# Running sums kept in one PSUM bank: the Winograd products of an output projection and an up projection

## The chip, the cores and the metric

The kernel runs on one NeuronCore of a Trainium2 chip. The metric is the device time of one execution in microseconds (us). Before the change it is 2968.75 us, the median of three runs (2968.43 to 2971.05).

The names of the engines are those of the profile: PE is the matrix engine (TensorE), PEld its weight loads, DVE the vector engine (VectorE), ACT the scalar engine (ScalarE), POOL GpSimd, and SP the engine whose queue issues most of the DMA transfers.

## The reference, cut to what matters

One layer of a hybrid encoder block for 512 tokens and a model width of 2048, in float32:

```
y  = RMSNorm(x) @ W_in                       # two recurrent groups of heads are fed from y
h  = x + concat[GDN(y), RWKV7(y)] @ W_out    # the output projection ("op")
h += CrossAttn(RMSNorm(h), RMSNorm(mem))
h += squared_relu(RMSNorm(h) @ W_up) @ W_down   # "up": 2048 -> 8192, "down": 8192 -> 2048
out = RMSNorm_final(h)
```

The change touches the two products `mixed @ W_out` (2048x2048) and `hn @ W_up` (2048x8192).

## The kernel before

Everything is held transposed: a tile has 128 features on the partitions and the 512 tokens along its free dimension. A float32 operand is split into two rounded parts, `hi` and `lo` (`split`, L130 and L131: ACT writes `hi`, DVE writes `lo = a - hi`), and a product is `hi·hi + hi·lo + lo·hi`, all three added up in PSUM.

Output projection and up are made of **units**: 8 units `op0` to `op7` and 32 units `up0` to `up31`, each a call of `strassen`. One unit makes a 256-feature by 512-token output. It is worked as a Winograd form of the 2x2 block product: the output is two feature halves (index 0 and 1) by two token halves, `HA` (tokens 0 to 255) and `HB` (256 to 511). Seven products replace eight. A product is named after its activation side, `B11`, `T1`, `T2`, `T3`, `T4`, `B22` or `B21`. That side lies ready in `comb[i][k]`, eight tiles of 512 columns: the `hi` part of 256 tokens in the first half, the `lo` part in the second. The weight side is one of the four blocks a11, a12, a21, a22 of 128x1024, loaded by DMA (L1305), or a combination of them: s1 = a21 + a22, s2 = s1 - a11, s4 = a12 - s2, and a11 - a21. DVE makes the combinations, and each product's weight side is then split by ACT and DVE.

A product is 24 multiplications of 128x128 by 256 columns. In `product` it is issued in one of two forms:

- **narrow**: for each of eight k, `hi` weights times `comb[:, HA]`, then the same weights times `comb[:, HB]`, both into the same 256 columns of the bank; then eight times `lo` weights times `comb[:, HA]`. 24 matmuls of 256 columns.
- **wide**: for each k, `hi` weights times all 512 columns of `comb`, into all 512 columns of the bank, so that two partial sums lie side by side; then the eight `lo` matmuls of 256 columns into the first half. 8 + 8 matmuls. Whoever reads the product must add both halves.

Units up1 to up30 are wide in all products; op1 to op6 in B11, T2 and T3 alone; op0, op7, up0 and up31 are narrow throughout.

Every product has a bank of its own. DVE adds the products up in SBUF, 256 columns at a time (`add`, L1336, one operand in PSUM): u1 = P1, u2 = u1 + P6, u3 = u2 + P7 and so on. A wide unit has 15 such additions and one ACT copy out of PSUM (L1354). `done` is called for each half tile as it is finished: in up it squares the ReLU on ACT and stores the tile (L1713 to L1716); in op it adds the input x and collects the sum of squares.

What sets the order: PE, DVE, ACT and SP each work through a queue in program order and wait on semaphores. In these stages the queues' order is made by the scheduler of the language layer when the program is built, from its own estimates, and not by the order of the source lines. Loaded blocks live in rotating buffers: `wraw` has three (a11 and a21 of each unit take turns in it), `wraw2` three (a22 and a12), `whi` and `wlo` two each, `ws` two. A load into a buffer waits for the last reader of what was in it.

Of the kernel before, what the change touches and what calls it, by code (L numbers as in the profile page):

```python
# [11 lines left out]
AF = mybir.ActivationFunctionType  # L12
ALU = mybir.AluOpType
# [4 lines left out]
P = 128  # L18
# [55 lines left out]
def build(tc, I, out):  # L74
    nc = tc.nc
# [42 lines left out]
    def psb(nm, tag="mx", bufs=2):  # L118
        return tile_of(ps, [P, 512], F32, tag, nm, bufs)

    def mm(o, l, r, start=True, stop=True):
        PE.matmul(o, l, r, start=start, stop=stop)  # L122

    def rsq(o, x, scale, eps):
        S.activation(o, x, AF.Ln, bias=eps, scale=scale)
# [1125 lines left out]
    def sl2(w=512):  # L1251
        cnt[0] += 1
        return ph.tile([P, 512], F32, tag="sl", name=f"sl{cnt[0]}", bufs=3)[:, 0:w]
# [17 lines left out]
    def sub(o, a, b):  # L1271
        V.tensor_tensor(out=o, in0=a, in1=b, op=ALU.subtract)
# [7 lines left out]
    def differ(i, e, o):  # L1280
        if i == T1:
            sub(e[:, HA], e[:, HB], e[:, HA])
        elif i == T2:
            sub(e[:, HA], o[:, HB], e[:, HA])
        elif i == T3:
            sub(e[:, HB], o[:, HB], e[:, HB])
        elif i == T4:
            sub(e[:, HA], e[:, HA], o[:, HA])

    def block(i, e, o):  # L1290
        return o[:, HB] if i == B22 else o[:, HA] if i == B21 else e[:, HB] if i == T3 else e[:, HA]

    def strassen(nm, pool, src, ks, done, used=None, first=False, wide=(), sums=None):

        w = len(ks) * P

        def raw(p_, tag, bufs, i):  # L1300
            cnt[0] += 1
            r = p_.tile([P, 1024], F32, tag=tag, name=f"{tag}_{cnt[0]}", bufs=bufs)[:, 0:w] \
                if p_ is pw else p_.tile([P, pool[1]], F32, tag=tag, name=f"{tag}_{cnt[0]}", bufs=bufs)[:, 0:w]
            if i is not None:
                nc.sync.dma_start(r, src[i])  # L1305
            return r

        def product(i, tag, a):
            cnt[0] += 1
            hi = pw.tile([P, 1024], F32R, tag="whi", name=f"whi{cnt[0]}", bufs=NWS)[:, 0:w]  # L1310
            lo = pw.tile([P, 1024], F32R, tag="wlo", name=f"wlo{cnt[0]}", bufs=NWS)[:, 0:w]
            split(a, hi, lo)
            pt = psb(f"{nm}_{i}", tag)
            pa_ = pt[:, HA]
            last = len(ks) - 1
            for zs in (range(last), range(last, last + 1)) if first else (range(last + 1),):
                for z in zs:
                    k, sl = ks[z], slice(z * P, z * P + P)
                    if i in wide:
                        mm(pt, hi[:, sl], comb[i][k], start=z == 0, stop=False)  # L1320
                    else:
                        mm(pa_, hi[:, sl], comb[i][k][:, HA], start=z == 0, stop=False)
                        mm(pa_, hi[:, sl], comb[i][k][:, HB], start=False, stop=False)
                for z in zs:
                    mm(pa_, lo[:, z * P:z * P + P], comb[i][ks[z]][:, HA], start=False, stop=z == last)
            if used:
                used(i)
            return (pa_, pt[:, HB]) if i in wide else (pa_,)

        def plus(o, a, p, op=ALU.add):  # L1330
            for x in p:
                add(o, a, x, op)
                a = o

        def add(o, a, b, op=ALU.add):
            V.tensor_tensor(out=o, in0=a, in1=b, op=op)  # L1336

        def wraw2(i):
            return raw(pool[0], "wraw2", 3, i)

        def ws():
            return raw(pool[0], "ws", 2, None)

        a11 = raw(pw, "wraw", NWR, 0)
        if first:
            a12, a22 = raw(pw, "wraw", NWR, 3), raw(pw, "wraw", NWR, 2)
            a21 = wraw2(1)
        else:
            a21 = raw(pw, "wraw", NWR, 1)
            a22, a12 = wraw2(2), wraw2(3)  # L1350
        p1 = product(B11, "mx", a11)
        c1 = sums[0] if sums else sl2()
        c11, c12 = u1, u4 = c1[:, HA], c1[:, HB]
        S.copy(u1, p1[0])  # L1354
        for x in p1[1:]:
            add(u1, u1, x)
        if first:
            p2 = product(B21, "mg", a12)
            p4 = product(T4, "mx", a22)
        s1 = ws()  # L1360
        add(s1, a21, a22)
        p5 = product(T1, "mg", s1)
        s2 = ws()
        add(s2, s1, a11, ALU.subtract)
        p6 = product(T2, "mm", s2)
        c2 = sums[1] if sums else sl2()
        c21, c22 = u3, u2 = c2[:, HA], c2[:, HB]
        plus(u2, u1, p6)
        if first:
            plus(c11, u1, p2)  # L1370
        plus(u4, u2, p5)
        add(a21, a11, a21, ALU.subtract)
        p7 = product(T3, "mm", a21)
        plus(u3, u2, p7)
        plus(c22, u3, p5)
        done(1, HB, c2)
        if not first:
            p4 = product(T4, "mx", a22)
        plus(c21, u3, p4, ALU.subtract)
        done(1, HA, c2)  # L1380
        s4 = ws()
        add(s4, a12, s2, ALU.subtract)
        p3 = product(B22, "mg", s4)
        plus(c12, u4, p3)
        done(0, HB, c1)
        if not first:
            p2 = product(B21, "mm", a12)
            plus(c11, u1, p2)
        done(0, HA, c1)

# [10 lines left out]
    def spread(*which):  # L1403
        for i, k in which:
            comb[i][k] = (btile if k < 3 or i == B21 and k < 6 else act_tile)(f"ob{i}_{k}")
            place(i, k, *pair[k])
# [114 lines left out]
    for p in range(8):  # L1521
        xs = [None, None]

        def used(i):
            if i == T1:
                if p == 0:
                    spread((B22, 6), (B22, 7))
                for j in (1, 0):
                    xs[j] = sl2()
                    nc.sync.dma_start(xs[j], I["xT"][:, 2 * p + j, :])  # L1530
            elif i == T2 and p == 0:
                spread((B21, 6), (B21, 7))
                sqsum.append(ph.tile([P, T], F32, tag="acc", name="acc1", bufs=1))
            if p == 7 and i in (T2, T3):
                for n in range(2) if i == T2 else range(2, 4):
                    second(n)

        def gained(j, half, c):
            if half is HB:
                return  # L1540
            V.tensor_tensor(out=c, in0=c, in1=xs[j], op=ALU.add)
            acc = sqsum[0]
            if p == 0 and j:
                S.activation(acc, c, AF.Square)
            else:
                sq = sl2()
                S.activation(sq, c, AF.Square)
                V.tensor_tensor(out=acc, in0=acc, in1=sq, op=ALU.add)

        strassen(f"op{p}", (pz, 1024), [I["w_out"][p, i] for i in range(4)], list(range(8)), gained, used,  # L1550
                 wide=(B11, T2, T3) if 0 < p < 7 else (), sums=hres[2 * p:2 * p + 2])
    pz_cm.__exit__(None, None, None)
    pl_cm = tc.tile_pool(name="pl", bufs=1, reuse_waits="tile")
    pl = pl_cm.__enter__()
# [153 lines left out]

    ahead = []
    for p in range(32):  # L1710
        def square(i, half, c):
            t = c[:, half]
            S.activation(t, t, AF.Relu)  # L1713
            S.activation(t, t, AF.Square)
            if half is HA:
                nc.scalar.dma_start(Ud[p][:, i, :], c)  # L1716

        def used(i):
            if p == 0 and i == B21:
                pt = psb("pss2")  # L1720
                mm(pt, ones, acc)
                V.tensor_scalar(out=rstd, in0=pt, scalar1=1.0 / 2048, scalar2=1e-6, op0=ALU.mult, op1=ALU.add)
            if 3 < p < 8 and i == T1:
                c = slice((p - 4) * P, (p - 3) * P)
                V.reciprocal(out=rstd[:, c], in_=rstd[:, c])
            if 7 < p < 16 and i in (B11, T3):
                f = p - 8
                if i == B11:
                    ahead.append(pu.tile([P, T], F32, tag="ur", name=f"ua{f}", bufs=1))
                    nc.sync.dma_start(ahead[f], Ud[f // 2][:, f % 2, :])  # L1730
                else:
                    V.tensor_tensor(out=ahead[f], in0=ahead[f], in1=rstd, op=ALU.mult)
                    nc.scalar.dma_start(Ud[f // 2][:, f % 2, :], ahead[f])
            if p == 31 and i in (T1, T2, T3):
                for f in (range(0, 3), range(3, 6), range(6, 8))[i - T1]:
                    usplit(f)

        strassen(f"up{p}", (pu, 1024), [I["w_up"][p, i] for i in range(4)], list(range(8)), square, used, p == 0,
                 range(7) if 0 < p < 31 else ())


    dcomb = {e: {i: [] for i in (T1, T2, T3, T4)} for e in range(1, 7)}
# [211 lines left out]
    pt = psb("pss4")  # L1954
# [126 lines left out]
```

## Time and profile before

| what | value |
|---|---|
| median of three runs | 2968.75 us |
| the profiled execution, first to last instruction | 2967.1 us |
| PE busy | 2938.2 us (99%) |
| DVE busy | 2323.9 us (78%) |
| ACT busy | 1520.1 us (51%) |
| stage op, first to last matmul | 1294.6 to 1455.4 us |
| stage up, first to last matmul | 1634.9 to 2263.2 us |

The span of the profiled execution is the time from its first to its last instruction. It is 1.65 us under the median of the three runs. In a row of a timeline the first column is the start in us from the start of the span, then the length in us, the engine, the source line, the operation, and what it writes from what; "x8" are eight instructions merged in one row, and brackets tell how long the engine had been idle and what ended that. The ends of matmuls are modelled and overlap the next start, so the pace of PE is read from starts. In a row of a group the busy time of the whole group stands behind the bar, then the mean duration of one in ns.

### The profile page before, as it was taken

The page shows a single profiled execution, that of the slowest core. Times are in us where ns is not written, and L with a number is a line of the kernel's source. Part 1 is how long each engine was busy: PE and PEld are TensorE (multiplying, and loading weights), DVE is VectorE, ACT ScalarE, POOL GpSimd, SP SyncE. Part 2 cuts the span into 40 slices and gives each one's busy share as a digit, 9 for nine tenths or more (in the row PEclk, how much of TensorE's full clock was granted, in tenths as well). Part 3 has the DMA queues.
Part 4 walks back from the last instruction along what each step waited for, and adds up shares of the span by engine and source line. Part 5 has one row for each costly group of instructions (what it writes and reads, how often), then busy time and mean ns, then how long its engine had stood idle before and what let it go on. Part 6 is the DMA issues. An engine that isn't in the chain of part 4 may idle for free.

```text
span 2967.1 us, 51025 instructions
## 1 busy us (share of the span) xinstructions
PE 2938.2 (99%) x20106; PEld 2515.2 (85%) x20106; DVE 2323.9 (78%) x3725; ACT 1520.1 (51%) x2271; POOL 215.2 (7%) x552
## 2 busy tenths in 40 slices
PE   9999999999999999999999999999999999999998
PEld 7877887887788888889988988888888888998887
DVE  7677676676778667679748999999999688888777
ACT  6455555555556555654436555555555343343334
POOL 0212302302312000000000000000000000000000
PEclk9999999999999999999999999999999999999999
DMA  5333332333435587864323445444445334333436
GB/s 179 111 87 85 101 93 81 102 92 82 132 89 166 168 278 250 259 231 136 100 86 100 146 153 170 136 142 135 136 135 177 110 108 139 128 114 114 135 121 185
DMA packets 229312, 407.35 MB, mean 137 GB/s; under 512 B 92168, under 2 KB 115980, under 8 KB 229072
## 3 DMA queue, kind: packets, MB, share of 16 engines
q1 hardware_dynamic: 212944, 375.77, 41.0%
q10 hardware_dynamic: 16128, 28.32, 2.6%
q8 instruction: 158, 2.59, 0.4%
q14 instruction: 82, 0.67, 0.1%
HBM read 354.32 MB, written 49.69 MB: 136 GB/s over the span
## 4 chain that ended last, share of the span: by engine, by line
PE 86%; DVE 6%; DMA 4%; POOL 2%; issue 2%; ACT 1%; SPq 0%; ACTq 0%; DVEq 0%; POOLq 0%
PE up L122 21%; PE py L251 20%; PE dn L122 14%; PE op L122 5%; PE d L122 4%; PE vp L122 3%; PE at L122 3%; PE sc L122 3%; PE kp L251 3%; PE kq L251 2%; DVE wlo L131 2%; POOL sr L251 2%; DVE h L1810 1%; PE vo L122 1%; DMA wraw<-in_wqT 1%
## 5 line engine op out<-in xcount | busy, mean ns | idle before, releaser
L130 ACT CAST whi<-wraw 128x1024 fp32r<-128x1024 f32 x372 | 391.4, 1052 | 567.6 <-PE dn L122 189.9
L131 DVE TENSOR_TENSOR wlo<-wraw,whi 128x1024 fp32r<-128x1024 f32 x372 | 453.9, 1220 | 64.4 <-ACT whi L130 60.9
L122 PE MATMUL up<-cb,whi 128*128 128x512 f32 (+1 forms) x1904 | 451.4, 380 | 0.0
L251 PE MATMUL py<-xhi,whi 128*128 128x512 f32 x928 | 374.2, 403 | 6.6 <-ACT xhi L251 6.6
L122 PEld LDWEIGHTS up<-cb,whi 128*128 128x128 f32 x1904 | 330.7, 189 | 54.9 <-issue 0.2
L251 PE MATMUL py<-xlo,whi 128*128 128x512 f32 x928 | 374.2, 403 | 0.0
L251 PE MATMUL py<-xhi,wlo 128*128 128x512 f32 x928 | 373.6, 403 | 0.1
L251 ACT CAST whi<-wraw 128x1024 fp32r<-128x1024 f32 (+1 forms) x180 | 188.0, 1044 | 211.9 <-PE py L251 133.1
L251 DVE TENSOR_TENSOR wlo<-wraw,whi 128x1024 fp32r<-128x1024 f32 (+1 forms) x180 | 220.9, 1227 | 87.7 <-ACT whi L251 86.5
L122 PEld LDWEIGHTS up<-cb,wlo 128*128 128x128 f32 x1792 | 244.1, 190 | 16.4
L122 PE MATMUL up<-cb,wlo 128*128 128x256 f32 x1792 | 251.1, 282 | 0.0
L122 PE MATMUL dn<-uh,whi 128*128 128x512 f32 x640 | 244.7, 391 | 0.8 <-ACT whi L130 0.8
L122 PE MATMUL dn<-ul,whi 128*128 128x512 f32 (+1 forms) x648 | 244.7, 388 | 0.0
L122 PE MATMUL dn<-uh,wlo 128*128 128x512 f32 (+1 forms) x640 | 235.1, 367 | 0.0
L251 PEld LDWEIGHTS py<-xhi,whi 128*128 128x128 f32 x928 | 175.3, 189 | 41.6 <-ACT xhi L251 7.0
L1336 DVE TENSOR_TENSOR sl<-sl,up 128x256 f32<-128x256 f32 x464 | 182.0, 414 | 35.0 <-PE up L122 31.8
L251 PEld LDWEIGHTS py<-xlo,whi 128*128 128x128 f32 x928 | 175.2, 189 | 37.3 <-issue 3.3
L251 PEld LDWEIGHTS py<-xhi,wlo 128*128 128x128 f32 x928 | 175.2, 189 | 35.2 <-issue 1.0
L130 ACT CAST whi<-ws 128x1024 fp32r<-128x1024 f32 x120 | 126.1, 1051 | 108.7 <-PE up L122 70.4
L1972 POOL TENSOR_TENSOR h<-h,rstd 128x256 f32<-128x256 f32 x5 | 3.4, 724 | 2012.6 <-ACT rstd L1966 2012.6
L131 DVE TENSOR_TENSOR wlo<-ws,whi 128x1024 fp32r<-128x1024 f32 x120 | 146.0, 1218 | 0.5 <-ACT whi L130 0.5
L122 PEld LDWEIGHTS dn<-uh,whi 128*128 128x128 f32 x640 | 120.2, 188 | 26.5 <-ACT whi L130 1.0
(882 smaller groups left out, 6420.7 us busy)
## 6 DMA issues: line engine op xcount, KB each, us to landing
wraw<-in_w_up SPq DMA_DIRECT2D x128, 512.0 KB, 3.5
wraw<-in_w_in SPq DMA_DIRECT2D x116, 512.0 KB, 3.7
wraw<-in_w_dn SPq DMA_DIRECT2D x96, 512.0 KB, 3.5
wraw<-in_wk SPq DMA_DIRECT2D x32, 512.0 KB, 4.0
wraw<-in_wqT SPq DMA_DIRECT2D x32, 512.0 KB, 5.3
wraw<-in_wv SPq DMA_DIRECT2D x32, 512.0 KB, 4.8
wraw<-in_wo SPq DMA_DIRECT2D x32, 512.0 KB, 5.6
wraw<-in_w_out SPq DMA_DIRECT2D x32, 512.0 KB, 3.4
```

Of the source, the lines that this page charges most:

```text
L122: PE.matmul(o, l, r, start=start, stop=stop)
L130: S.copy(hi, src)
L131: V.tensor_tensor(out=lo, in0=src, in1=hi.bitcast(F32), op=ALU.subtract)
L251: f(*a, **k)
L1336: V.tensor_tensor(out=o, in0=a, in1=b, op=op)
L1810: V.tensor_tensor(out=h, in0=h, in1=two(src), op=ALU.add)
L1972: GP.tensor_tensor(out=h, in0=h, in1=rstd[:, HB], op=ALU.mult)
```

## The change

All products of all units become wide, and a unit uses three banks (x, y, z) for its seven products. A product whose sum another one continues is added into the same bank, and the sum in between is read out in passing:

- x: P1, read out (u1); plus P6, read out (u2); plus P7, read out (u3); minus P4, read out. T4's activation side changes its sign (`o - e` for `e - o`), so that P4 can be added.
- z: P5, read out; plus P3, read out.
- y: P2, read out.

Two helpers read a bank: `take` (an ACT copy of one half, then a DVE addition of the other) starts an output block, and `gain` (two DVE additions) adds to one. The order of the products becomes B11, T1, T2, B21, T3, B22, T4. s4 is made in a12's own buffer. The last read of a unit (`rest`) and its `done(1, ...)` are kept back until the next unit has issued its first product and s1. `done` is called for a whole tile of 512 columns.

```
-    def strassen(nm, pool, src, ks, done, used=None, first=False, wide=(), sums=None):
+    def strassen(nm, pool, src, ks, done, used=None, first=False, sums=None):
...
+                    mm(pt, hi[:, z * P:z * P + P], comb[i][ks[z]], start=start and z == 0, stop=False, again=True)
...
+        def take(o, pt):
+            S.copy(o, pt[:, HB])
+            V.tensor_tensor(out=o, in0=pt[:, HA], in1=o, op=ALU.add)
+
+        def gain(o, pt):
+            for part in (HA, HB):
+                V.tensor_tensor(out=o, in0=o, in1=pt[:, part], op=ALU.add)
...
+        product(B11, a11, x, True)
...
+        s1 = combine(None, a21, a22, ALU.add)
+        while kept:
+            kept.pop(0)()
+        c1 = tile2(0)
+        product(T1, s1, z, True)
+        take(c1[:, HA], x)
+        s2 = combine(None, s1, a11)
+        product(T2, s2, x)
+        c2 = tile2(1)
+        take(c2[:, HB], z)
...
+            product(B21, a12, y, True)
+            combine(a21, a11, a21)
+            take(c1[:, HB], x)
+            product(T3, a21, x)
+            gain(c1[:, HA], y)
+            combine(a12, a12, s2)
+            product(B22, a12, z)
+            gain(c2[:, HB], x)
+            product(T4, a22, x)
+            gain(c1[:, HB], z)
+            done(0, c1)
+
+            def rest():
+                take(c2[:, HA], x)
+                done(1, c2)
+        kept.append(rest)
```

In the changed kernel `take` has the lines L1325 (ACT) and L1326 (DVE), `gain` L1330, `combine` L1334, and the loads L1307.

The built program tells the order of each queue. In units up8 to up30 DVE's queue, from the end of one unit into the next, reads as follows (the unit n is the one that begins):

```
gain  c1.HB of n-1 <- z, first half     (waits for B22 of n-1)
split lo of B11, unit n                 (last reader of a11 of n)
gain  c1.HB of n-1 <- z, second half
split lo of T1, unit n
take  c2.HA of n-1 <- x of n-1
s1 of n+1    = a21 + a22                (waits for the loads of n+1)
a11 - a21 of n+1, written over a21
split lo of T2, unit n
take  c1.HA of n <- x                   (PE waits for this one before T2 of n)
split lo of B21, unit n
```

In up5 to up7 the take of c1.HA stands ahead of the split of T2; there is an `ua` multiplication (L1738) ahead of s1 as well. The kernel before has s1 and a11 - a21 behind the lo splits of T2 and T3. In the op units of the changed program the first matmul of the next unit's B11 (two of them once) stands ahead of T4 in PE's queue.

More of the change, by code (lines that the diff above doesn't have):

```diff
@@ L119, in psb, with mm @@
         return tile_of(ps, [P, 512], F32, tag, nm, bufs)
-    def mm(o, l, r, start=True, stop=True):
-        PE.matmul(o, l, r, start=start, stop=stop)
+    def mm(o, l, r, start=True, stop=True, again=False):
+        PE.matmul(o, l, r, start=start, stop=stop, skip_group_check=again)
     def rsq(o, x, scale, eps):
@@ L1287, in differ @@
         elif i == T4:
-            sub(e[:, HA], e[:, HA], o[:, HA])
+            sub(e[:, HA], o[:, HA], e[:, HA])
     def block(i, e, o):
         return o[:, HB] if i == B22 else o[:, HA] if i == B21 else e[:, HB] if i == T3 else e[:, HA]
-    def strassen(nm, pool, src, ks, done, used=None, first=False, wide=(), sums=None):
+    kept = []
+    def strassen(nm, pool, src, ks, done, used=None, first=False, sums=None):
         w = len(ks) * P
@@ L1306, in raw, with product @@
             return r
-        def product(i, tag, a):
+        def product(i, a, pt, start=False):
             cnt[0] += 1
@@ L1312, in product @@
             split(a, hi, lo)
-            pt = psb(f"{nm}_{i}", tag)
-            pa_ = pt[:, HA]
             last = len(ks) - 1
@@ L1317, in product, with combine, tile2 @@
                 for z in zs:
[L1318 to L1323, printed above, removed]
+                    mm(pt, hi[:, z * P:z * P + P], comb[i][ks[z]], start=start and z == 0, stop=False, again=True)
                 for z in zs:
-                    mm(pa_, lo[:, z * P:z * P + P], comb[i][ks[z]][:, HA], start=False, stop=z == last)
+                    mm(pt[:, HA], lo[:, z * P:z * P + P], comb[i][ks[z]][:, HA], start=False, stop=z == last, again=True)
             if used:
                 used(i)
[L1328 to L1335, printed above, removed]
+        def take(o, pt):
[4 more added lines that the diff above has]
+                V.tensor_tensor(out=o, in0=o, in1=pt[:, part], op=ALU.add)
+        def combine(o, a, b, op=ALU.subtract):
+            o = o or raw(pool[0], "ws", 2, None)
             V.tensor_tensor(out=o, in0=a, in1=b, op=op)
+            return o
         def wraw2(i):
             return raw(pool[0], "wraw2", 3, i)
-        def ws():
-            return raw(pool[0], "ws", 2, None)
+        def tile2(j):
+            return sums[j] if sums else sl2()
+        x, y, z = (psb(f"{nm}_{t}", tag) for t, tag in (("x", "mx"), ("y", "mm"), ("z", "mg")))
         a11 = raw(pw, "wraw", NWR, 0)
@@ L1350, in strassen @@
             a22, a12 = wraw2(2), wraw2(3)
[L1351 to L1356, printed above, removed]
-        if first:
[L1358 to L1365, printed above, removed]
@@ L1366, in strassen @@
-        c2 = sums[1] if sums else sl2()
-        c21, c22 = u3, u2 = c2[:, HA], c2[:, HB]
-        plus(u2, u1, p6)
-        if first:
[L1370 to L1389, printed above, removed]
+        product(B11, a11, x, True)
+        if first:
+            v = psb(f"{nm}_v", "scr", 1)
+            product(B21, a12, y, True)
+            product(T4, a22, v, True)
+        s1 = combine(None, a21, a22, ALU.add)
+        while kept:
+            kept.pop(0)()
+        c1 = tile2(0)
@@ new lines, in strassen, with rest @@
+        product(T1, s1, z, True)
[4 more added lines that the diff above has]
+        take(c2[:, HB], z)
+        if first:
+            gain(c1[:, HA], y)
+            s4 = combine(a12, a12, s2)
+            combine(a21, a11, a21)
+            product(B22, s4, z)
+            take(c1[:, HB], x)
+            product(T3, a21, x)
+            gain(c1[:, HB], z)
+            done(0, c1)
+            S.copy(c2[:, HA], v[:, HB])
+            V.tensor_tensor(out=c2[:, HA], in0=c2[:, HA], in1=v[:, HA], op=ALU.add)
+            def rest():
+                for half in (HA, HB):
+                    gain(c2[:, half], x)
+                done(1, c2)
+        else:
+            product(B21, a12, y, True)
+            combine(a21, a11, a21)
+            take(c1[:, HB], x)
+            product(T3, a21, x)
+            gain(c1[:, HA], y)
+            combine(a12, a12, s2)
+            product(B22, a12, z)
+            gain(c2[:, HB], x)
+            product(T4, a22, x)
+            gain(c1[:, HB], z)
+            done(0, c1)
+            def rest():
+                take(c2[:, HA], x)
+                done(1, c2)
@@ L1526, in used @@
                 if p == 0:
-                    spread((B22, 6), (B22, 7))
+                    spread((B21, 6), (B21, 7))
                 for j in (1, 0):
@@ L1531, in used @@
             elif i == T2 and p == 0:
-                spread((B21, 6), (B21, 7))
+                spread((B22, 6), (B22, 7))
                 sqsum.append(ph.tile([P, T], F32, tag="acc", name="acc1", bufs=1))
@@ L1536, in used, with gained @@
                     second(n)
-        def gained(j, half, c):
-            if half is HB:
-                return
+        def gained(j, c, p=p, xs=xs):
             V.tensor_tensor(out=c, in0=c, in1=xs[j], op=ALU.add)
             acc = sqsum[0]
-            if p == 0 and j:
+            if p == 0 and not j:
                 S.activation(acc, c, AF.Square)
@@ L1550, in build @@
         strassen(f"op{p}", (pz, 1024), [I["w_out"][p, i] for i in range(4)], list(range(8)), gained, used,
-                 wide=(B11, T2, T3) if 0 < p < 7 else (), sums=hres[2 * p:2 * p + 2])
+                 sums=hres[2 * p:2 * p + 2])
+    kept.pop()()
     pz_cm.__exit__(None, None, None)
@@ L1710, in build, with square @@
     for p in range(32):
[L1711 to L1716, printed above, removed]
+        def square(i, c, p=p):
+            S.activation(c, c, AF.Relu)
+            S.activation(c, c, AF.Square)
+            nc.scalar.dma_start(Ud[p][:, i, :], c)
         def used(i):
@@ L1736, in used @@
                     usplit(f)
-        strassen(f"up{p}", (pu, 1024), [I["w_up"][p, i] for i in range(4)], list(range(8)), square, used, p == 0,
-                 range(7) if 0 < p < 31 else ())
+        strassen(f"up{p}", (pu, 1024), [I["w_up"][p, i] for i in range(4)], list(range(8)), square, used, p == 0)
+    kept.pop()()
     dcomb = {e: {i: [] for i in (T1, T2, T3, T4)} for e in range(1, 7)}
```

## The prediction

> **What bounds the kernel now.** I read the page first, then the busy time of the two changed stages, then PE's list of waits.
>
> ```profile
> span 2967.1 us, 51025 instructions
> ...
> PE 2938.2 (99%) x20106; PEld 2515.2 (85%) x20106; DVE 2323.9 (78%) x3725; ACT 1520.1 (51%) x2271; POOL 215.2 (7%) x552
> ...
> wraw<-in_w_up SPq DMA_DIRECT2D x128, 512.0 KB, 3.5
> ```
>
> ```profile
> 1294.60:1455.40 160.80, 160.32 (x1200) 153.68 (x1199) 151.60 (x202) 75.47 (x92) 0.00 (x0) 1.00 0.41 135
> 1635.10:2263.30 628.20, 628.17 (x3700) 557.00 (x3699) 588.79 (x851) 343.10 (x526) 0.00 (x0) 1.00 0.45 146
> ```
>
> ```profile
> PE d L122 <- DVE wlo L131: 3.4, 10, 0.3
> PE kp L251 <- DVE wlo L251: 2.4, 4, 1.1
> ...
> PE op L122 <- ACT whi L130: 0.2, 1, 0.2
> PE op L122 <- DVE wlo L131: 0.2, 1, 0.2
> ```
>
> The two rows of stretches are op and up: length, then busy time of PE, PEld, DVE, ACT and POOL, the granted clock, DMA. PE is busy in all of both stages, and in its list of waits (us in total, times, longest) the op units stand with 0.4 us and no up unit stands at all. So PE's own matmuls set the time of both stages; DVE, busy for 94% of each (151.60 of 160.80, 588.79 of 628.20), is close behind but ends no wait. Two things can move the time: a cheaper stream of matmuls, or a wait of PE that is not there now. No idle time of PE is there to be won.
>
> **Fewer matmuls.** Narrow pairs become single wide matmuls:
>
> ```profile
> L122 PE MATMUL op<-ob,whi 128*128 128x256 f32 x608 | 79.2, 283 | 0.2 <-ACT whi L130 0.2
> ...
> L122 PE MATMUL up<-cb,whi 128*128 128x256 f32 x224 | 30.8, 285 | 0.0
> ```
>
> ```profile
> 1344.36 2.00 PE L122 MATMUL op<-ob,whi 128*128 128x512 f32 x8
> 1346.20 1.12 PE L122 MATMUL op<-ob,wlo 128*128 128x256 f32 x8
> 1347.15 2.08 PE L122 MATMUL op<-ob,whi 128*128 128x256 f32 x16
> 1349.08 1.12 PE L122 MATMUL op<-ob,wlo 128*128 128x256 f32 x8
> ```
>
> (608 + 224) / 2 = 416 pairs. The lengths in the rows overlap, so I go by starts: eight wide matmuls take 1346.20 - 1344.36 = 1.84 us, eight pairs 1349.08 - 1347.15 = 1.93 us. That is 0.09 us for eight, 0.010 to 0.011 us for a pair. The gain is 416 x 0.0102 = **4.2 us**, all of it on PE and so on the path.
>
> **Less work on DVE.** A wide up unit had 15 additions of 256 columns and gets 10; the starts 1793.60 and 1793.94 below put 0.34 us on one that is followed at once. That is 1.7 us less for each of 30 units, and three more ACT copies. I cost it at **0**: no wait of PE in up ends on DVE. In op the additions go from 74 to 80 (8 units of 10), the ACT copies from 8 to 32. Squaring whole tiles takes four ACT passes where eight stood; ACT is busy for 343 of 628 us. The stores become as large as before; their number stays.
>
> **A new wait in up8 to up30.** T2 is added into bank x, which still holds u1; PE may not start it before DVE's take of c1.HA has read the bank. DVE's queue, as the built program has it, puts s1 and a11 - a21 of the next unit and the lo split of T2 ahead of that take. The rows for their pace, from one unit of before (B11 starts at 1793.40, T1 at 1796.19, T2 at 1798.99):
>
> ```profile
> 1792.45 1.12 PE L122 MATMUL up<-cb,wlo 128*128 128x256 f32 x8
> ...
> 1793.40 2.00 PE L122 MATMUL up<-cb,whi 128*128 128x512 f32 x8
> ...
> 1793.60 0.42 DVE L1336 TENSOR_TENSOR sl<-sl,up 128x256 f32<-128x256 f32 x1 [0.31 <-PE up L122]
> ...
> 1793.94 1.22 DVE L131 TENSOR_TENSOR wlo<-ws,whi 128x1024 fp32r<-128x1024 f32 x1
> ...
> 1796.19 2.00 PE L122 MATMUL up<-cb,whi 128*128 128x512 f32 x8
> ...
> 1798.01 1.22 DVE L1336 TENSOR_TENSOR ws<-wraw,wraw 128x1024 f32<-128x1024 f32 x1
> ...
> 1798.23 1.05 ACT L130 CAST whi<-wraw 128x1024 fp32r<-128x1024 f32 x1 [0.85 <-PE up L122]
> ...
> 1798.99 2.00 PE L122 MATMUL up<-cb,whi 128*128 128x512 f32 x8
> 1799.32 1.23 DVE L131 TENSOR_TENSOR wlo<-wraw,whi 128x1024 fp32r<-128x1024 f32 x1
> 1800.46 1.22 DVE L1336 TENSOR_TENSOR wraw<-wraw,wraw 128x1024 f32<-128x1024 f32 x1
> 1801.60 0.68 DVE L1732 TENSOR_TENSOR ua<-ua,rstd 128x512 f32<-128x512 f32 x1
> ```
>
> A product lasts 2.80 us (1793.40 to 1796.19). A DVE instruction of 1024 columns is followed by the next after 1.14 us (1799.32, 1800.46, 1801.60). An addition that waits for a product starts 0.20 us after the next product has started (1793.60), the lo split behind it 0.34 us later, and that one ends at 1795.16, 1.76 us after the product's start.
>
> When does s1 of the next unit get its a21? The buffer of a21 is that of a11 of the unit that begins, whose last reader is B11's lo split, and the load goes out right behind it, as it does now:
>
> ```profile
> 1792.08 1.21 DVE L131 TENSOR_TENSOR wlo<-wraw,whi 128x1024 fp32r<-128x1024 f32 x1
> ...
> 1793.32 0.33 SPq L1305 DMA_DIRECT2D wraw<-in_w_up  x1
> ```
>
> The load starts 0.03 us after the split's end (1793.29). Today s1 comes at 1798.01, 4.69 us after it, and seldom waits. In the changed queue s1 stands a product earlier. With B11's start as 0:
>
> - B11's lo split stands behind an addition that waits for the end of B22, so it keeps to T4's start at -2.80: it ends at -2.80 + 1.76 = -1.04. The load goes out at -1.01.
> - It lands 3.5 us later (last row of the first fence, a median; I take 3.55 for a few late ones): 2.54. s1 starts at 2.57 with the 0.03 us that a wait takes there (1793.57, where the PE row ends, to 1793.60).
> - s1 ends at 3.79. a11 - a21 overwrites a21 and waits for that: 3.82. T2's lo split 1.14 later, 4.96; the take 1.14 later, 6.10, and 0.42 long, 6.52. PE starts at about 6.56.
> - PE was ready for T2 at 2 x 2.80 = 5.59.
>
> So PE waits 0.97 us in each of the 23 units: **22.3 us**. Behind the waiting take stand the split of B21 and all that follows in DVE's queue; PE itself is what is late, and no later product makes it up, since PE has no idle time to give back. The next unit's load is again tied to T4 and B11 and repeats it.
>
> The bounds of this cost. Below: were the load there at once, s1 would start behind T1's lo split and the take of c2.HA. T1's cast waits for the hi matmuls of T4 and ends at T4's start + 3.09, the pace of the cast row against 1796.19; that is 0.29, and then 0.03 + 1.14 + 0.34 give s1 at 1.80 instead of 2.57. PE waits 0.20 us, 4.6 us in all. Above: s1 of before has 4.69 us of grace, and how often that was too little is in these two rows:
>
> ```profile
> DVE ws L1336 <- DMA wraw<-in_w_up: 0.8, 2, 0.6
> ```
>
> ```profile
> 2092.23 1.23 DVE L1336 TENSOR_TENSOR ws<-wraw,wraw 128x1024 f32<-128x1024 f32 x1 [0.59 <-DMA wraw<-in_w_up]
> ```
>
> Two waits of 0.8 us together in 31 units: landings beyond 4.69 us are rare. With 4.69 in every unit the wait would be 2.11 us, 48.5 us in all. I take the median load, since the loads before a21 are spaced as widely as now.
>
> **op and the ends.** In op1 to op7 the next unit's first matmul stands ahead of T4. Its hi part needs the buffer that B22's hi matmuls leave: cast from 1798.23 to 1799.28 against a product that started at 1796.19, 3.09 after it and 3.13 with PE's start, where PE arrives after 2.80. That is 0.33 us in each of seven units: **2.3 us**, between 0, if that cast starts 0.33 us earlier there, and 7 x 1.05 = 7.4, if the whole of it showed. In op the take precedes T2's split. In up1 to up7 it does too, and 1.14 us less leaves no wait in most: 6.56 - 1.14 = 5.42 is before 5.59. up0 and up31 have the splits of other stages in DVE's queue ahead of a take: 0 to 2 us, **1.0** taken.
>
> **Sum:** -4.2 + 22.3 + 2.3 + 1.0 = +21.4 us. The profiled execution would go from 2967.1 to 2988.5 us, the median, 1.65 us above it, from 2968.75 to **2990.2 us**, 0.7% slower. About 0.2% (6 us) is what a measurement of this kernel can tell from no change.
>
> **Rivals.**
>
> 1. *The bank is read in time* (not slower). If the take of c1.HA is out by 5.55, PE never waits for it and only the matmuls count: 2968.75 - 4.2 = 2964.5 us. It decides at a landing of 2.54 - 0.97 + 1.01, about 2.6 us after the issue, with T1's split out of the way too. The median of 3.5 speaks against it, and so does the 0.20 us that is left with no load to wait for. 4%.
> 2. *The load is not what is late* (another view of the buffers, an earlier issue): only the queue's 0.20 us, -4.2 + 4.6 + 2.3 + 1.0 = +3.7, 2972.5 us. 4%.
> 3. *DVE was the hidden bound*, and 1.7 us less in each of 30 units is 51 us gained: 2918 us. Its 94% speaks for it, the absence of any up row among PE's waits against it. 2%.
> 4. *Late loads*: landings towards 4.69 us and PE waits up to 2.1 us, +47, 3016 us. The DMA row of up and the two rare waits speak against it. 4%.
> 5. *The clock falls.* If each of the 23 waits cost the clock for the length of one product, at half speed, that adds 23 x 2.80 = 64 us: 3055 us. Against it:
>
> ```profile
> core 0: 2967.1 us, clock 0.999
> ```
>
> The granted clock is full although PE waited 1.1 us at a time in kp and ten times in d (second fence of waits). 3%. The Trainium skill's page "TensorE: Matmul & The Clock Gate", section "A second HAM failure mode: psum-queue depth-cycling", speaks for this rival: it tells of a kernel whose many small idle times between groups of matmuls, as it cycled through PSUM banks, made the clock swing between half and full. The trace of before does not show that, with fewer and shorter waits than I expect here.
>
> **How the numbers follow.** The forecast has 83%, by itself 2979 (a load of 3.2 us: 23 x 0.62 = 14.3, no wait in op or at the ends) to 3001 (4.0 us: 23 x 1.42 = 32.7, the rest as in the sum). The range 2975 to 3004 reaches a little beyond on both sides and leaves out rivals 1 to 5. Slower: 83 + 4 + 3 = 90%. Same: rivals 1 and 2, 8%. Faster: rival 3, 2%.
>
> **What would show it.** Right: in the profile after, a row "PE up waits for DVE" of some 23 times and 0.9 to 1.0 us each, at the first matmul of T2; DVE's s1 waiting for the load of w_up 0.7 us in each of these units; PE waiting for ACT seven times 0.3 us in op; 416 matmuls fewer; the granted clock at 1.00. Wrong: the take in the trace ends before T1 does; or s1 starts without a wait; or PE's waits are spread over other products (T3 or T4 on bank x), which would mean that another read is late.

## The result and the profile after

The changed kernel takes 3005.11 us (median of 4 runs, 3004.43 to 3009.22) against 2968.59 us (4 runs, 2968.26 to 2971.05): a ratio of 1.0125, 95% interval 1.0110 to 1.0139. It is slower, as forecast, but by 36 us where I had 21: it lies 1.1 us above the upper end of my range.

The page of the profile after, the rows that answer to those of before:

```profile
span 3003.2 us, 50138 instructions
...
PE 2943.2 (98%) x19690; PEld 2495.0 (83%) x19690; DVE 2282.9 (76%) x3589; ACT 1527.1 (51%) x2263; POOL 212.7 (7%) x552
...
wraw<-in_w_up SPq DMA_DIRECT2D x128, 512.0 KB, 3.2
```

PE has 416 matmuls fewer (20106 to 19690), as counted. The span is 36.1 us longer. The two stages, as stretches (length, then PE, PEld, DVE, ACT, POOL, granted clock, DMA):

```profile
1293.50:1457.10 163.60, 159.89 (x898) 138.18 (x897) 151.71 (x207) 80.83 (x115) 0.00 (x0) 1.00 0.41 132
1636.60:2298.30 661.70, 634.93 (x3587) 552.38 (x3586) 543.16 (x706) 343.44 (x492) 0.00 (x0) 1.00 0.42 139
```

Up was 628.2 us and is 661.7; op was 161.0 and is 163.6. DVE works 46 us less in up (588.79 to 543.16), and the stage is longer all the same. The clock is full. PE's list of waits (us in total, times, longest) has what was not there before:

```profile
PE up_x L122 <- DVE sl L1326: 24.8, 27, 2.8
...
PE op_x L122 <- ACT whi L130: 1.3, 7, 0.2
PE op_x L122 <- DVE h L1326: 1.1, 2, 0.7
...
PE up_z L122 <- ACT whi L130: 0.7, 1, 0.7
PE up_y L122 <- ACT whi L130: 0.7, 1, 0.7
```

27 waits for the take of c1.HA (L1326), where 23 were forecast. These idle times go by modelled ends of matmuls, so from here on I go by starts. This is one of the 23 units, from the timeline after, all engines (some rows left out):

```profile
2152.85 2.00 PE L122 MATMUL up_x<-cb,whi 128*128 128x512 f32 x8
...
2155.43 1.23 DVE L1334 TENSOR_TENSOR ws<-wraw,wraw 128x1024 f32<-128x1024 f32 x1 [0.69 <-DVE sl L1326]
...
2155.64 2.00 PE L122 MATMUL up_z<-cb,whi 128*128 128x512 f32 x8
...
2156.69 1.23 DVE L1334 TENSOR_TENSOR wraw<-wraw,wraw 128x1024 f32<-128x1024 f32 x1
...
2157.83 1.22 DVE L131 TENSOR_TENSOR wlo<-ws,whi 128x1024 fp32r<-128x1024 f32 x1
...
2158.97 0.42 DVE L1326 TENSOR_TENSOR sl<-up_x,sl 128x256 f32<-128x256 f32 x1
...
2159.44 1.69 PEld L122 LDWEIGHTS up_x<-cb,whi 128*128 128x128 f32 x8 [1.05 <-DVE sl L1326]
2159.44 2.11 PE L122 MATMUL up_x<-cb,whi 128*128 128x512 f32 x8 [0.84 <-DVE sl L1326]
...
2161.39 1.11 PE L122 MATMUL up_x<-cb,wlo 128*128 128x256 f32 x8
2162.22 1.70 PEld L122 LDWEIGHTS up_y<-cb,whi 128*128 128x128 f32 x8
2162.34 2.00 PE L122 MATMUL up_y<-cb,whi 128*128 128x512 f32 x8
```

Of the 20 units with the usual wait this is the one that waits longest. Counted from B11's start (2152.85): s1 at 2.58, a11 - a21 at 3.84, the lo split of T2 at 4.98, the take at 6.12, T2 at 6.59, where PE was ready at 5.58. The prediction had 2.57, 3.82, 4.96, 6.10, 6.56 and 5.59. (The bracket at s1 names DVE's own instruction, which had ended 0.69 us before; what s1 then still waits for is its load. In 17 of the units up8 to up30 the list names that:)

```profile
DVE ws L1334 <- DMA wraw<-in_w_up: 10.9, 17, 1.5
```

One thing in this unit was not in the forecast. T2's eight hi matmuls take 2161.39 - 2159.44 = 1.95 us by starts, and 1.84 everywhere else. The two PEld rows suggest why: before an undelayed product the weight load starts 0.12 us ahead of the matmul (2162.22, 2162.34), beside the matmul before it; after a wait the first load starts with the wait's end, at 2159.44 like the matmul row, and nothing covers it. Each wait costs **0.11 us** more than its own length; that the uncovered weight load is the reason is read from these rows, and no run takes it apart.

Stretch by stretch, from start to start (us). The border between op0 and op1 is where op1's B11 goes on behind T4 of op0: two matmuls of that B11 (0.46 us) and its late start ahead of T4 (0.46 us with the restart) lie in op0's row.

| stretch | before | after | longer by | forecast |
|---|---|---|---|---|
| op0 | 21.40 | 22.53 | 1.1 | -0.6 |
| op1 to op7 | 139.56 | 141.05 | 1.5 | 2.3 - 2.5 = -0.2 |
| up0, up31 | 41.57 | 43.08 | 1.5 | 1.0 - 1.1 = -0.1 |
| up1 to up3 | 58.66 | 58.68 | 0.0 | 0 |
| up4 to up7 | 78.21 | 85.24 | 7.0 | 0 |
| up8 to up30 | 449.73 | 474.67 | 24.9 | 22.3 |
| both stages | 789.13 | 825.25 | 36.1 | 21.4 |

The forecast's 4.2 us for 416 pairs are spread here over the stretches that had narrow products. The rest of the run is as long as it was. Of the 24.9 us in up8 to up30, 22.5 are waits ahead of T2 (0.73 to 1.01 us in 20 units, median of all 0.85; 1.75, 1.85 and 1.93 in three) and 23 x 0.11 = 2.5 are the restarts. In the three (up17, up23, up30) s1 starts 4.3 to 4.5 us after its load went out, in the others 3.3 to 3.6; the loads go out at the same spacing, and why these three land late stays open.

In up4 to up7 T2 is late by 2.99, 1.40, 1.50 and 0.74 us. DVE's timeline after, in up4 (B11 starts at 1716.95) and up5 (1739.59):

```profile
1721.06 1.23 DVE L1334 TENSOR_TENSOR ws<-wraw,wraw 128x1024 f32<-128x1024 f32 x1 [2.17 <-DMA wraw<-in_w_up]
1723.30 0.69 DVE L1738 TENSOR_TENSOR ua<-ua,rstd 128x512 f32<-128x512 f32 x1 [1.02 <-DMA ua<-ud]
1723.91 1.22 DVE L131 TENSOR_TENSOR wlo<-ws,whi 128x1024 fp32r<-128x1024 f32 x1
1725.05 0.42 DVE L1326 TENSOR_TENSOR sl<-up_x,sl 128x256 f32<-128x256 f32 x1
...
1742.35 0.69 DVE L1738 TENSOR_TENSOR ua<-ua,rstd 128x512 f32<-128x512 f32 x1 [0.87 <-DMA ua<-ud]
1743.70 1.23 DVE L1334 TENSOR_TENSOR ws<-wraw,wraw 128x1024 f32<-128x1024 f32 x1 [0.66 <-DMA wraw<-in_w_up]
1744.96 1.23 DVE L1334 TENSOR_TENSOR wraw<-wraw,wraw 128x1024 f32<-128x1024 f32 x1
1746.10 0.42 DVE L1326 TENSOR_TENSOR sl<-up_x,sl 128x256 f32<-128x256 f32 x1
```

And the two loads that go out ahead of up5, on SP's queue:

```profile
1737.82 0.33 SPq L1736 DMA_DIRECT2D ua<-ud  x1
1738.58 0.33 SPq L1307 DMA_DIRECT2D wraw<-in_w_up  x1
```

In up5 the order is the one that the forecast had: s1, a11 - a21, the take, and T2's split behind it. The multiplication of `ua` ahead of s1 is over at 1743.04, 0.66 us before s1 starts, so it is not what holds s1. What holds s1 is its load: it went out at 1738.58, 1.01 us before B11's start as in all these units, and s1 starts 5.12 us after that, where the forecast has 3.58. From s1 to the take it is 2.40 us, as forecast. Up6 and up7 read the same, with s1 5.21 and 4.45 us after its load's issue. In all three a load of `ua` had gone out 0.8 to 1.0 us ahead. In up4 s1 is as late (5.12 us), and there the `ua` multiplication, late by its own load, and T2's split do stand between s1 and the take.

### The profile page after: what moved, and what is told of

Its sections match the earlier page's. It is cut to its first block, busy times and chain, and to the rows that moved or that the text cites. A ratio compares the mean times of both kernels' runs of the same rounds, so it can differ in the third digit from the quotient of the medians.

```text
span 3003.2 us, 50138 instructions
## 1 busy us (share of the span) xinstructions
PE 2943.2 (98%) x19690; PEld 2495.0 (83%) x19690; DVE 2282.9 (76%) x3589; ACT 1527.1 (51%) x2263; POOL 212.7 (7%) x552
## 4 chain that ended last, share of the span: by engine, by line
PE 84%; DVE 9%; DMA 3%; issue 2%; ACT 1%; POOL 0%; SPq 0%; DVEq 0%; ACTq 0%
PE py L251 21%; PE dn L122 14%; PE up_x L122 11%; PE up_z L122 5%; PE d L122 3%; PE kq L251 3%; PE vp L122 3%; PE at L122 3%; PE sc L122 3%; PE up_y L122 3%; DVE wlo L131 3%; PE kp L251 3%; PE op_x L122 2%; PE vo L122 1%; DVE h L1816 1%
## 5 line engine op out<-in xcount | busy, mean ns | idle before, releaser
L130 ACT CAST whi<-wraw 128x1024 fp32r<-128x1024 f32 x412 | 432.2, 1051 | 628.4 <-PE dn L122 196.0
L131 DVE TENSOR_TENSOR wlo<-wraw,whi 128x1024 fp32r<-128x1024 f32 x412 | 502.9, 1221 | 62.5 <-ACT whi L130 59.3
L251 DVE TENSOR_TENSOR wlo<-wraw,whi 128x1024 fp32r<-128x1024 f32 (+1 forms) x180 | 222.4, 1236 | 87.7 <-ACT whi L251 86.4
L122 PE MATMUL up_x<-cb,whi 128*128 128x512 f32 x1016 | 257.9, 395 | 25.0 <-DVE sl L1326 24.8
L122 PEld LDWEIGHTS up_x<-cb,whi 128*128 128x128 f32 x1016 | 182.4, 189 | 63.7 <-DVE sl L1326 30.2
L122 PEld LDWEIGHTS up_x<-cb,wlo 128*128 128x128 f32 x1016 | 138.8, 190 | 10.0
L122 PE MATMUL up_x<-cb,wlo 128*128 128x256 f32 x1016 | 142.1, 282 | 0.0
L122 PEld LDWEIGHTS dn<-ul,whi 128*128 128x128 f32 x648 | 121.2, 188 | 24.7
L122 PE MATMUL d<-dt,whi 128*128 128x256 f32 x768 | 139.9, 283 | 0.0
L122 PEld LDWEIGHTS dn<-uh,wlo 128*128 128x128 f32 x640 | 120.3, 188 | 20.7 <-DVE wlo L131 0.6
```

What stands on the lines that cost most here:

```text
L122: PE.matmul(o, l, r, start=start, stop=stop, skip_group_check=again)
L130: S.copy(hi, src)
L131: V.tensor_tensor(out=lo, in0=src, in1=hi.bitcast(F32), op=ALU.subtract)
L251: f(*a, **k)
```

## The experiments

**The theories.** *Queue*: PE waits because DVE's take of c1.HA, which frees bank x for T2, stands behind s1 (late by its load), a11 - a21 and T2's split. *Bank*, the rival: to add products up in one bank that is read in between costs time by itself, in whatever order. *Load alone* or *place alone*: of s1's lateness, only the transfer or only the place in the queue counts. The last two runs ask what holds op and the first up units.

**e1_dve_order: the take first.** In each unit DVE's s1 (of the next unit) and T2's split are put behind the take.

```
+        def behind():
+            return tc.issue_after(first_read[0].ins) if first_read else nullcontext()
...
+        with behind():
+            s1 = combine(None, a21, a22, ALU.add)
...
+        first_read[:] = [take(c1[:, HA], x)]
         s2 = combine(None, s1, a11)
-        product(T2, s2, x)
+        with behind():
+            product(T2, s2, x)
```

> The changed kernel with one thing different: VectorE does the take of c1.HA before s1 of the next unit and before T2's split. The work is the same. Queue theory (PE waits for T2 because that take stands in VectorE's queue behind s1, which waits for its load, and behind T2's lo split): the product ahead of T2 loses the excess seen in the trace after, 25.0 us in up8 to up30 and 7.1 us in up4 to up7; T2's own split, now behind the take, may bring back some 0.5 us in a few units, and op keeps its waits. 2974 to 2982 us. Rival, the bank theory (to add products up in one bank that is read in between slows the matmuls or the reads themselves): the order is not the cause, 2995 to 3005 us, and the waits of T2 stay.

Measured: 2976.04 us (10 runs) against 2969.37 us before (27 runs), ratio 1.0022, interval 1.0013 to 1.0031. The stretches op and up of this kernel, and DVE's timeline in one unit (B11 starts at 2051.14, T2 at 2056.72):

```profile
1292.40:1455.80 163.40, 159.84 (x898) 138.01 (x897) 152.67 (x207) 82.29 (x116) 0.00 (x0) 1.00 0.42 131
1635.40:2268.40 633.00, 629.52 (x3587) 551.13 (x3586) 535.88 (x706) 347.51 (x492) 0.00 (x0) 1.00 0.44 145
```

```profile
2055.55 0.42 DVE L1326 TENSOR_TENSOR sl<-up_x,sl 128x256 f32<-128x256 f32 x1 [2.52 <-ACT sl L1325]
2055.89 1.22 DVE L131 TENSOR_TENSOR wlo<-ws,whi 128x1024 fp32r<-128x1024 f32 x1
2057.02 1.22 DVE L1334 TENSOR_TENSOR ws<-wraw,wraw 128x1024 f32<-128x1024 f32 x1
```

The same instructions in another order: up is 28.7 us shorter (661.7 to 633.0). DVE now has the bank read 0.75 us before T2 is due (2055.97, 2056.72) and stands idle for 2.52 us ahead of that read. Every product of up12 to up30 starts 2.79 us after the one before. The bank theory is out: the sums are still chained in one bank and read in between. (Up is still 4.8 us longer than before: in five units up to up10 the next B11 stands ahead of T4 in PE's queue and is late, in up8 T2's lo split is, and up31 takes 1.6 us more.)

**e2_no_first_read: the read left out.**

```
-        take(c1[:, HA], x)
...
-            gain(c1[:, HA], y)
+            take(c1[:, HA], y)
```

> The changed kernel without the take of c1.HA out of bank x: c1.HA starts with a take of bank y instead, so P1 is left out of that output block. The matmuls, the loads and the split order remain; VectorE has one addition of 256 columns and one copy less in each unit. Three of the four reads between products of one bank are still there (x before T3, x before T4, z before B22). Queue theory: T2 waits for nothing any more, 25.0 + 7.1 us go in up, some 2 us in up31 and op; 2966 to 2973 us. Bank theory: a quarter to a third of the 36 us goes with one read of four, 2993 to 2997 us.

Measured: 2975.60 us (10 runs), ratio 1.0022, interval 1.0013 to 1.0031; 2.6 us above what the queue theory said, far below the bank theory. Up, PE's wait, and DVE in one unit (T2 starts at 1740.13):

```profile
1632.70:2268.30 635.60, 630.16 (x3588) 550.90 (x3587) 521.37 (x644) 343.87 (x491) 0.00 (x0) 1.00 0.44 144
```

```profile
PE up_x L122 <- DVE wlo L131: 4.3, 4, 1.8
```

```profile
1739.01 0.69 DVE L1737 TENSOR_TENSOR ua<-ua,rstd 128x512 f32<-128x512 f32 x1 [2.58 <-DMA ua<-ud]
1740.21 1.23 DVE L1334 TENSOR_TENSOR ws<-wraw,wraw 128x1024 f32<-128x1024 f32 x1 [0.51 <-DMA wraw<-in_w_up]
...
1742.62 1.22 DVE L131 TENSOR_TENSOR wlo<-ws,whi 128x1024 fp32r<-128x1024 f32 x1
```

T2 waits no more in up8 to up30, though bank x is still read before T3 and before T4. Up is still 7.4 us longer than before. Most of that are the units with `ua`: with no take to wait for, it is T2's own lo split that stands behind ua and s1, and the lo matmuls wait for it. Outside both stages PE has one wait that the changed kernel has not: 1.6 us for a lo split where the down projection begins.

**e3_half_load: a shorter load, the same order.**

```
-            a21 = raw(pw, "wraw", NWR, 1)
+            a21 = raw(pw, "wraw", NWR, None)
+            nc.sync.dma_start(a21[:, 0:w // 2], src[1][:, 0:w // 2])
+            nc.gpsimd.memset(a21[:, w // 2:w], 0.0)
```

> The changed kernel with half of each a21 loaded (256 KB instead of 512 KB; the other half is set to zero by POOL, so half of that weight block is left out). The order of every queue stays. If the load is what makes s1 late (my step: 2.54 us after the start of B11, against 1.80 without a load to wait for), the wait of T2 falls from a median of 0.85 us to about 0.2 us: 23 x 0.65 = 15 us less in up8 to up30 and 3 to 5 us in up4 to up7, 2985 to 2990 us. If the place in the queue alone is what counts, the wait stays and so does the time: 3002 to 3006 us. If the restart after a wait costs the same however short the wait is, T2's row stays at 2.11 us wherever a wait is left.

Measured: 2986.67 us (4 runs), ratio 1.0060, interval 1.0047 to 1.0074. One unit of it (B11 starts at 2099.59), and s1's waits in DVE's list over up8 to up30:

```profile
2101.40 1.22 DVE L1334 TENSOR_TENSOR ws<-wraw,wraw 128x1024 f32<-128x1024 f32 x1
...
2104.92 0.41 DVE L1326 TENSOR_TENSOR sl<-up_x,sl 128x256 f32<-128x256 f32 x1
...
2105.39 2.11 PE L122 MATMUL up_x<-cb,whi 128*128 128x512 f32 x8
```

```profile
DVE ws L1334 <- DMA wraw<-in_w_up: 1.1, 3, 0.5
```

s1 starts at 1.81 us after B11, with no wait, and T2 at 5.80, 0.22 us late. That is the lower bound of the prediction, worked out there as 1.80 and 0.20. Up8 to up30 take 459.8 us against 474.7: 14.9 us less, where I had expected 15. The place in the queue alone leaves 0.22 us, the late load makes the other 0.63 of the median. The row is still 2.11 us long: the restart is paid in full even after a short wait. (The list of DMA issues puts the halves at 3.1 us to landing, by which s1 would still wait in most units. But it knows the landing of only 7 of the 31 halves, all of them before up8. By s1's own starts, a half is there within 2.8 us in 13 of the 23 units up8 to up30.)

In up4 to up7 the 3 to 5 us expected did not come (86.4 us against 85.2). The order is not the same there: in this program T2's split stands ahead of the take in up4, up5 and up7, and in up5 a `ua` multiplication as well, which waits for its own load until 4.89 us after B11's start. And the shorter load is not always early: in up7, where three loads went out within 4.12 us and none of `ua` near them, s1 starts 4.89 us after the half load's issue.

**e4_both_orders: T4 before the next B11 on PE as well.**

```
+                    m_ = mm(pt[:, HA], lo[:, z * P:z * P + P], comb[i][ks[z]][:, HA], start=False, stop=z == last, again=True)
+            last_mm[:] = [m_]
...
-        product(B11, a11, x, True)
+        with tc.issue_after(last_mm[0].ins) if last_mm else nullcontext():
+            product(B11, a11, x, True)
```

> The kernel of the first experiment with one order more: on PE, T4 of a unit stands before B11 of the next, so that no cast for a hi part is late. Queue theory: T2's waits go (32 us) and op's seven starts of B11 too (3.2 us), and what is left is the gain of 416 wide matmuls (4.2 us) less one or two waits of a microsecond in up0 and the first units: 2964 to 2968 us against 2968.6 for the kernel before, so 0.0 to 0.15% faster than before. Bank theory: 2985 us or more.

Measured: 2973.17 us (11 runs), ratio 1.0011, interval 1.0002 to 1.0020: 5 us above my expectation, and slightly slower than before. Its stretches op and up:

```profile
1295.10:1456.80 161.70, 158.50 (x898) 138.10 (x897) 152.75 (x207) 81.77 (x115) 0.00 (x0) 1.00 0.42 134
1636.30:2267.70 631.40, 628.98 (x3588) 551.10 (x3588) 536.27 (x706) 347.52 (x492) 0.00 (x0) 1.00 0.45 145
```

Up1 to up30 are clean but for two units (1.4 and 0.3 us late). What eats the gain of the wide matmuls are the ends: op0 takes 22.5 us (21.4 before), op7's B22 waits 1.17 us, up31 takes 21.9 (20.2 before).

**e5_both_orders_s4: a buffer for s4 at the ends.**

```
-            combine(a12, a12, s2)
+            a12 = combine(None if nm in ("op7", "up31") else a12, a12, s2)
```

> The kernel with both orders, and in op7 and up31 a12 - s2 goes to a buffer of its own instead of over a12, so that it need not wait until the split of B21 has read a12. In the trace with both orders B22 waits 1.17 us for its cast in op7 and 0.86 + 0.11 us in up31, and those casts wait for a12 - s2. If that chain is the cause, 2.1 us go: 2971 us against 2973.2 for both orders alone and 2969.4 for the kernel before. If VectorE is simply full of the next stage's splits there, B22 is as late as it was and the time stays at 2973 us.

Measured: 2972.94 us (11 runs) against 2968.93 us before (15 runs), ratio 1.0013, interval 1.0004 to 1.0022. Stretches, and from PE's list two waits in op and one where the down projection (dn) begins:

```profile
1293.80:1454.70 160.90, 158.34 (x897) 138.16 (x896) 152.27 (x207) 81.22 (x115) 0.00 (x0) 1.00 0.42 132
1634.30:2263.70 629.40, 628.13 (x3587) 551.31 (x3586) 535.37 (x705) 345.73 (x491) 0.00 (x0) 1.00 0.45 146
```

```profile
PE dn L122 <- DVE wlo L131: 1.8, 1, 1.8
...
PE op_z L122 <- ACT whi L130: 1.4, 2, 1.0
...
PE op_x L122 <- DVE h L1331: 0.6, 1, 0.6
```

In the trace both waits of B22 are gone (op7's products all take 2.79 us, and up31's B22 too), so the chain through a12 was their cause. The time is the 2973 us of the rival all the same. The two stages have 2.6 us less than in e4, but 1.8 us of that come back right behind them, as a wait for a lo split at the start of down that e4 does not have, and the medians of the two cannot be told apart. Op and up together now take 790.4 us against 789.1 before; op0 (23.0 for 21.4) and up31 (21.0 for 20.2) still give back what op1 to op7 gain (138.0 for 139.6). No version here beats the kernel before.

**e6_pe_order: PE's order alone.** The diff of e4, without that of e1.

> The changed kernel with only PE's order different: T4 of a unit stands before B11 of the next. My step for op said that the seven late starts come of the hi cast that B11 waits for when it follows B22 at once: they cost 0.35 us and a restart of 0.11 us each in the trace after, so op falls from 163.6 us to 160.4 us, and PE's row of seven waits for ACT in op is gone. Up has T4 first already and stays within 0.5 us of 661.7 us. Rival: VectorE's late reads hold op just as well, and op falls by less than 1 us.

Measured: 3010.68 us, one run. Op, and PE's waits in op:

```profile
1296.90:1460.20 163.30, 159.24 (x897) 138.15 (x896) 151.74 (x207) 80.59 (x114) 0.00 (x0) 1.00 0.41 133
```

```profile
PE op_x L122 <- DVE h L1331: 1.6, 4, 0.6
```

The rival was right. The seven waits of B11 for ACT are gone, and op is as long as in the changed kernel: in four units T4 now waits for DVE's second read of bank x (L1331), and in op4 T2 for its take (0.9 us). Neither order alone shortens op (163.4 in e1, 163.4 here by starts, 163.6 with none); both together do (161.7). Two engines were late there by about the same (T4 loses 0.56 us here in each of three units, B11 0.46 us in the changed kernel, restarts included), which a list that names the last one cannot show. This execution's span is 5.7 us above the changed kernel's; 3.6 of that lie in up (665.3), with long waits in up4 and up6 (3.1 and 2.1 us), the rest outside both stages. It is a single run, and the four of the changed kernel alone spread over 4.8 us.

**e7_no_ahead: no ua.**

```
-            if 7 < p < 16 and i in (B11, T3):
+            if False and i in (B11, T3):
```

> The changed kernel without the early scaling of eight tiles of the up output (ua: load, multiplication by rstd and store are left out, so those tiles stay unscaled). In the trace after up1 to up3 have no wait of T2, up4 to up7 have 3.0, 1.4, 1.5 and 0.7 us, and ua multiplications stand ahead of the take there. If ua is what is late in up4 to up7 and nothing else, T2 waits nowhere in up1 to up7 and up takes 654.5 us (661.7 less 7.1). If the queue without ua is just that of up8 to up30, with s1, a11 - a21 and T2's split ahead of the take, every unit from up1 on waits 0.85 + 0.11 us: 7 x 0.96 = 6.7 us come for the 7.1 that go, and up takes 661 us.

Measured: 3006.12 us, one run. Up, and DVE's timeline in up5 (B11 starts at 1740.30, its load went out at 1739.29):

```profile
1636.40:2299.60 663.20, 636.59 (x3588) 553.55 (x3587) 538.58 (x698) 343.42 (x492) 0.00 (x0) 1.00 0.40 132
```

```profile
1742.65 1.23 DVE L1334 TENSOR_TENSOR ws<-wraw,wraw 128x1024 f32<-128x1024 f32 x1 [0.47 <-DVE sl L1326]
...
1745.06 1.22 DVE L131 TENSOR_TENSOR wlo<-ws,whi 128x1024 fp32r<-128x1024 f32 x1
1746.19 0.42 DVE L1326 TENSOR_TENSOR sl<-up_x,sl 128x256 f32<-128x256 f32 x1
```

Neither expectation holds as a whole. In up1 to up3 T2 does not wait, with ua or without; in up4 to up7 it waits without it too, by 1.95, 0.78, 0.78 and 0.83 us, and in up4 B21 by another 1.66. But two things changed in up5 to up7, and they work against each other. The load is back in time: s1 starts 3.37, 3.36 and 3.41 us after its load's issue, where the changed kernel has 5.12, 5.21 and 4.45. And the program has another order there, that of up8 to up30, with T2's split ahead of the take. With the changed kernel's order the bank would be read by 2.36 + 2.40 + 0.42 = 5.18 us after B11's start, before T2 is due at 5.59 (an estimate from these rows). So this run does not price ua in the order of the changed kernel. It shows that the load of a21 lands late in up5 to up7 with ua's work and not without; whether ua's load or its store is what delays it is not taken apart. In up4, where three loads went out within 4.12 us in both programs, s1 comes 4.5 us after its load's issue without ua and 5.1 with it.

## Why the prediction was right and wrong

- **What bounds the kernel: right.** PE had no idle time to give back. 46 us less of DVE's work in up brought nothing, and each wait of PE showed in full.
- **The gain of 416 wide matmuls: right.** A product that was narrow took 2.88 us and takes 2.79 wherever it waits for nothing.
- **The wait of T2 in up8 to up30: right** in place and cause, and near in size: 22.5 us of waits against 22.3. That the totals agree this well is luck: the load was 0.12 us quicker than the 3.55 us I took in the typical unit (0.85 for 0.97), and three late loads made up for that. e1, e2 and e3 show the cause from three sides.
- **Not costed: the restart after a wait.** 0.11 us each, 2.5 us in up8 to up30, 0.4 in up4 to up7, some 1.5 in op and at the ends.
- **The step that failed: "In up1 to up7 it does too, and 1.14 us less leaves no wait in most."** The sum behind it, 6.56 - 1.14 = 5.42, keeps the 3.55 us that a load takes in a typical unit. In up1 to up3 T2 has no wait. In up5 to up7 the order was read rightly, but s1 started 5.12, 5.21 and 4.45 us after its load's issue instead of 3.58, behind a load of `ua` that the forecast put at nothing; in up5 that moves the end of the wait from 5.42 to 6.98 after B11's start, 1.40 us past T2's turn. In up4 the load was as late, as three loads went out within some 4 us and one of `ua` behind them, and the order was read wrongly: T2's split and the `ua` multiplication stand ahead of the take. Together 7.0 us where I had 0, half of what I missed. The issues ahead of up4:

```profile
1711.82 4.45 SPq L1307 DMA_DIRECT2D wraw<-in_w_up  x3
```

The third went out 4.12 us after the first. "I take the median load, since the loads before a21 are spaced as widely as now" was true of the steady units alone.

- **Mis-sized: op and the ends.** 2.3 us for the seven starts of B11 became 0.46 x 7 = 3.2 with the restart; T2's waits in op4 and op5 (the list's 1.1 us for L1326) were not foreseen; op0 was left out of the ends (some 0.8 us over the forecast, without what belongs to op1), and up0 and up31 cost 1.6 us more than I had.
- **The rivals.** Late loads (rival 4) came in three of the 23 units and in up4 to up7, not throughout. The clock (rival 5) did not fall: 1.00 in both stages, with 27 waits 20 us apart. The rule of the Trainium skill's page "TensorE: Matmul & The Clock Gate", section "A second HAM failure mode: psum-queue depth-cycling", which spoke for rival 5, is not borne out here. Rival 3 is out by the DVE row of up.

## What to carry to other kernels

When two sums are chained in one PSUM bank, the read between them is on PE's path: look where it stands in the reading engine's queue, and what the instructions ahead of it wait for. In-order queues make an early instruction that waits for a transfer into a wait of everything behind it; moving two such instructions back took away 28.7 of the 33.5 us by which up had grown. And take a load's time unit by unit, not from a typical one: in up4 to up7 loads that shared the queue with others came 0.9 to 1.6 us later than forecast, and these four units made half of the forecast's error.

## What the runs showed of the hardware that was not expected

- A wait of PE costs 0.11 us beyond its length, whether it lasts 0.22 us or 1 us (2.11 us for a row that else takes 2.00). By the rows of weight loads, the first one after the wait is not hidden beside a matmul; this reason is not tested.
- A 512 KB load that is there 3.3 to 3.6 us after its issue in 20 of 23 steady units took 4.5 to 5.2 us in up5 to up7, where a 256 KB load had gone out 0.8 to 1.0 us ahead, and 3.4 us in the same units with that work left out. With three loads in 4.12 us it took 4.5 us (up4 of e7).
